# Rotary embedding of 16 x 512 x 1024: rows of a tile taken in pairs, tables on a second queue, the last tile stored whole

## The chip, the cores and the metric

One core of a Trainium2 chip. The metric is the device time of one execution in microseconds (us); lower is better. A run over 1.5% above the fastest of its kernel counts as slow and is left out of the ratios. "DVE" is the vector engine, "Pool" in the profile is GpSimd, "ACT" is ScalarE, "PE" the tensor engine and "SP" the engine that issues most transfers. Sixteen DMA engines move the data.

## The reference

```python
batch, seq, dim = 16, 512, 1024        # float32, 16 heads of 64
x1, x2 = x[..., :32], x[..., 32:]      # per head
out = concatenate([x1 * cos - x2 * sin, x1 * sin + x2 * cos], axis=-1)
# cos and sin: [512, 32], the same for all batches and heads
```

In and out are 33.55 MB each; the tables are 64 KB each.

## The kernel before

A tile is two batches: 128 partitions with eight sequence rows of 1024 values each, 4 MB. There are eight tiles and five buffers. Each output row is `x * cos + swapped(x) * sin`, where `swapped` exchanges the halves of each head and the sign is in the table. DVE makes the cosine product into PSUM, GpSimd the sine product into SBUF (`b`), and DVE adds the two. In two of the eight rows PE adds instead, by a product with the identity, and ScalarE copies the sum out; for row 0 DVE makes the sine product too.

```python
FIRST = (3, 8); LAST_OUT = (4, 8); SMALL = (15, 14, 12, 8)
PE_ROWS = ((0, 4), (0, 4)); DVE_B = ((0,), (0,))

load(0, 0, FIRST[0])                                # all on SP's queue
nc.sync.dma_start(out=sin_sb, in_=sin_v)
nc.sync.dma_start(out=cos_sb, in_=cos_v)
for lo, hi in zip(FIRST, FIRST[1:]): load(0, lo, hi)
for t in range(1, BUFS): load(t)
# ... tables spread over 128 partitions by PE, then into `sns` by DVE ...

for t in range(NT):
    for k in range(KK):                             # one row of 1024 at a time
        if not own:   nc.gpsimd.tensor_tensor(out=halves(b), in0=swapped(r, nh), in1=over_heads(sk), op=ALU.mult)
        if k in PE_ROWS[t % 2]:
            # two cosine products of 512, [own: one sine product on DVE], two PE additions, two ACT copies
        else:
            nc.vector.tensor_tensor(out=pairs(ps), in0=pairs(r), in1=cos_b(k, 2 * nh), op=ALU.mult)
            pending.append((r, ps, b))              # later: r = ps + b on DVE
        if k == 0 and t > 0: finish(t - 1)          # sums, then the store on SP's queue
    if t == NT // 2 - 1: # four tiny loads on ScalarE's queue that nothing uses
finish(NT - 1)                                      # last tile: rows 0-3, then rows 4-7
```

SP issues all loads and stores of `x` in the order loads 0 to 4, stores 0 to 2, loads 5 to 7, stores 3 to 7.

## Time and profile before

| | before |
|---|---|
| time, median of 3 runs | 162.39 us (162.34 to 162.41) |
| span of the profile | 160.7 us |
| moved by the main queue | 67.24 MB, in use 97.9% of the span |
| DVE busy, Pool busy | 141.4 us, 130.3 us |
| DVE on data | 10.75 to 151.88 us |
| last store issued, landed | 151.96, 159.8 us |

How to read it: ask first which resource has no idle time from beginning to end. A high busy share is not enough; DVE is busy 88% and is idle only at the ends, yet it has finished almost 9 us before the span does. The lines of the profile that carry this are in the prediction.

### The profile page before, as it was taken

The page shows a single profiled execution, that of the slowest core. Times are in us where ns is not written, and L with a number is a line of the kernel's source. Part 1 is how long each engine was busy: PE and PEld are TensorE (multiplying, and loading weights), DVE is VectorE, ACT ScalarE, POOL GpSimd, SP SyncE. Part 2 cuts the span into 40 slices and gives each one's busy share as a digit, 9 for nine tenths or more (in the row PEclk, how much of TensorE's full clock was granted, in tenths as well). Part 3 has the DMA queues.
Part 4 walks back from the last instruction along what each step waited for, and adds up shares of the span by engine and source line. Part 5 has one row for each costly group of instructions (what it writes and reads, how often), then busy time and mean ns, then how long its engine had stood idle before and what let it go on. Part 6 is the DMA issues. An engine that isn't in the chain of part 4 may idle for free. (4 is left out here: it accounts for less than half of the span.)

```text
span 160.7 us, 531 instructions
## 1 busy us (share of the span) xinstructions
PE 62.1 (39%) x71; PEld 20.0 (12%) x71; DVE 141.4 (88%) x142; ACT 20.0 (12%) x33; POOL 130.3 (81%) x62
## 2 busy tenths in 40 slices
PE   3146370536217250709045540918063722735000
PEld 0112010202011110202020200211020201120000
DVE  1059999999999999999999999999999999999800
ACT  0201120021102020111102020202001110202000
POOL 1039999999999999999999899999999799940000
PEclk9999958576956776595555555555555585587655
DMA  5999999999999999999999999999999999999994
GB/s 190 398 408 473 392 490 424 392 481 432 392 432 473 394 432 473 400 400 498 408 400 465 441 400 434 457 416 424 465 408 424 473 408 416 465 416 412 416 432 192
DMA packets 2852, 67.26 MB, mean 419 GB/s; under 512 B 418, under 2 KB 546, under 8 KB 546
## 3 DMA queue, kind: packets, MB, share of 16 engines
q1 hardware_dynamic: 2752, 67.24, 97.9%
q10 hardware_dynamic: 98, 0.00, 0.0%
q14 instruction: 2, 0.02, 0.0%
HBM read 33.69 MB, written 33.55 MB: 419 GB/s over the span
## 5 line engine op out<-in xcount | busy, mean ns | idle before, releaser
L168 POOL TENSOR_TENSOR b<-xt,sns 128x1024 f32<-128x1024 f32 x56 | 129.6, 2354 | 11.6 <-DVE sns L111 9.2
L186 DVE TENSOR_TENSOR pd<-xt,tab 128x1024 f32<-128x1024 f32 x48 | 58.1, 1225 | 0.8
L148 DVE TENSOR_TENSOR xt<-pd,b 128x1024 f32<-128x1024 f32 x48 | 58.3, 1217 | 0.0
L181 PE MATMUL ps<-xt,ident 128*128 128x512 f32 x32 | 29.6, 1082 | 49.0 <-issue 38.4
L181 PE MATMUL ps<-b,ident 128*128 128x512 f32 x32 | 29.0, 1061 | 29.6 <-DVE ps L174 27.0
L182 ACT COPY xt<-ps 128x512 f32<-128x512 f32 x32 | 18.7, 585 | 120.4 <-PE ps L181 120.4
L174 DVE TENSOR_TENSOR ps<-xt,tab 128x512 f32<-128x512 f32 x32 | 20.6, 687 | 0.0
L181 PEld LDWEIGHTS ps<-xt,ident 128*128 128x128 f32 x32 | 9.4, 324 | 68.3 <-issue 63.7
L181 PEld LDWEIGHTS ps<-b,ident 128*128 128x128 f32 x32 | 9.2, 316 | 49.6 <-issue 25.6
L179 DVE TENSOR_TENSOR xt<-xt,tab 128x1024 f32<-128x1024 f32 x8 | 9.8, 1221 | 0.4
L110 DVE TENSOR_SCALAR sns<-tab 128x256 f32<-128x256 f32 x1 | 0.4, 425 | 8.1 <-PE tab L108 8.1
L107 PE MATMUL tab<-b,spread 64*128 64x256 f32 x2 | 1.2, 697 | 5.0 <-DMA b<-in_sin_dram 5.0
L182 ACT ACT_TABLE_LOAD x1 | 1.3, 1283 | 7.1 <-DMA xt<-in_x_dram 7.1
L97 PE MATMUL ps<-zero 128*128 128x512 bf16 x3 | 1.5, 623 | 1.2 <-DVE zero L94 1.2
L107 PEld LDWEIGHTS tab<-b,spread 64*128 64x128 f32 x2 | 0.5, 306 | 5.9 <-issue 5.9
L108 PE MATMUL tab<-b,spread 64*128 64x256 f32 x2 | 1.1, 632 | 0.0
L94 DVE MEMSET zero<- 128x256 uint32 x1 | 0.3, 272 | 0.9 <-PEq L211 0.9
L108 PEld LDWEIGHTS tab<-b,spread 64*128 64x128 f32 x2 | 0.7, 334 | 0.2
L106 DVE COPY spread<-ident 64x64 f32<-64x64 f32 x2 | 0.3, 182 | 0.2 <-POOL ident masks.py:199 0.2
L97 PEld LDWEIGHTS <-zero 128*128 128x128 bf16 x3 | 0.3, 124 | 1.5 <-DVE zero L94 1.2
masks.py:197 POOL MEMSET ident<- 128x128 f32 x1 | 0.2, 204 | 0.3 <-POOLq L211 0.3
L111 DVE COPY sns<-tab 128x256 f32<-128x256 f32 x1 | 0.4, 414 | 0.0
(6 smaller groups left out, 0.9 us busy)
## 6 DMA issues: line engine op xcount, KB each, us to landing
xt<-in_x_dram SPq DMA_DIRECT2D x7, 4096.0 KB, 29.1
out_dram<-xt SPq DMA_DIRECT2D x7, 4096.0 KB, 27.8
out_dram<-xt SPq DMA_DIRECT2D x2, 2048.0 KB, 8.4
xt<-in_x_dram SPq DMA_DIRECT2D x1, 2560.0 KB
xt<-in_x_dram SPq DMA_DIRECT2D x1, 1536.0 KB, 6.3
b<-in_sin_dram SPq DMA_DIRECT2D x1, 64.0 KB, 6.3
b<-in_cos_dram SPq DMA_DIRECT2D x1, 64.0 KB, 6.1
spare<-in_sin_dram ACTq DMA_DIRECT2D x1, 0.9 KB, 5.7
```

The source lines that it names most:

```text
L97: nc.tensor.matmul(out=ps, lhsT=zero[:, :P], rhs=zero, start=True, stop=True)
L107: nc.tensor.matmul(out=sin_t, lhsT=spread, rhs=sin_sb, start=True, stop=True)
L108: nc.tensor.matmul(out=cos_t, lhsT=spread, rhs=cos_sb, start=True, stop=True)
L110: nc.vector.tensor_scalar_mul(out=sns[:, :, 0, :], in0=sin_k, scalar1=-1.0)
L111: nc.vector.tensor_copy(out=sns[:, :, 1, :], in_=sin_k)
L148: nc.vector.tensor_tensor(out=r, in0=ps, in1=b, op=ALU.add)
L168: nc.gpsimd.tensor_tensor(out=halves(b), in0=swapped(r, nh), in1=over_heads(sk), op=ALU.mult)
L174: nc.vector.tensor_tensor(out=pairs(ps), in0=pairs(rc), in1=cos_b(k, BANK // half), op=ALU.mult)
L179: nc.vector.tensor_tensor(out=halves(r), in0=halves(r), in1=swapped_signed(k), op=ALU.mult)
L181: nc.tensor.matmul(out=ps, lhsT=ident, rhs=rhs, start=False, stop=True, skip_group_check=True)
L182: nc.scalar.copy(out=rc, in_=ps)
L186: nc.vector.tensor_tensor(out=pairs(ps), in0=pairs(r), in1=cos_b(k, 2 * nh), op=ALU.mult)
```

## The change

The intent: fewer, longer instructions on DVE and GpSimd (six of eight rows in pairs), tables that needn't wait behind the first load, and one transfer less at the end. The diff, cut to its core ("..." marks a cut; the comments are added here):

```diff
-B_BUFS = 6
-PE_ROWS = ((0, 4), (0, 4))
-DVE_B = ((0,), (0,))
-FIRST = (3, 8)
-LAST_OUT = (4, 8)
-SMALL = (15, 14, 12, 8)
+ROW_OWN, ROW_PE = 0, 3
+PAIRS = ((1, 2), (4, 5), (6, 7))
+FIRST = (2, 3, 8)
+LAST_OUT = (8,)
+EXTRA = 4
...
-    nc.sync.dma_start(out=sin_sb, in_=sin_v)
-    nc.sync.dma_start(out=cos_sb, in_=cos_v)
+    nc.scalar.dma_start(out=sin_sb, in_=sin_v)
+    nc.scalar.dma_start(out=cos_sb, in_=cos_v)
...
+    spare = fixed.tile([1, EXTRA, 16], FP32)
+    for i in range(EXTRA):
+        nc.sync.dma_start(out=spare[:1, i], in_=sin_v[:1, :16])
...
+    cos_product(own_ps, rows(0, ROW_OWN), ROW_OWN)
     for t in range(NT):
-        for k in range(KK):                      # one row at a time ... (cut)
+        first, second, third = PAIRS
+        b1 = sin_rows(t, first[0], 2)            # GpSimd, 2048 elements
+        p1 = pair_product(t, first[0])           # DVE, 2048 elements
+        r0 = rows(t, ROW_OWN)
+        own_product(r0)                          # DVE, 1024
+        for ps, r in zip(parts(own_ps), parts(r0)):
+            pe_add(ps, swapped(r))
+        nc.scalar.copy(out=r0, in_=own_ps)
+        b3 = sin_rows(t, ROW_PE, 1)
+        b2 = sin_rows(t, second[0], 2)
+        pair_sum(*p1, b1)                        # DVE, 2048
+        h0, h1 = zip(parts(rows(t, ROW_PE)), parts(b3))
+        pe_half(ROW_PE, *h0)                     # DVE 512, PE, ACT
+        p2 = pair_product(t, second[0])
+        b1 = sin_rows(t, third[0], 2)
+        pair_sum(*p2, b2)
+        pe_half(ROW_PE, *h1)
+        p1 = pair_product(t, third[0])
+        if t + 1 < NT:
+            cos_product(own_ps, rows(t + 1, ROW_OWN), ROW_OWN)
+        pair_sum(*p1, b1)
+        stores(t)
```

The buffers for `b` become three of twice the size, and the sum of each row 0 is made in one PSUM tile of 1024.

More of the change, by code (lines that the diff above doesn't have):

```diff
@@ L61 @@
     xp = ctx.enter_context(tc.tile_pool(name="xp", bufs=BUFS))
-    bp = ctx.enter_context(tc.tile_pool(name="bp", bufs=B_BUFS))
+    bp = ctx.enter_context(tc.tile_pool(name="bp", bufs=3))
     pfix = ctx.enter_context(tc.tile_pool(name="pfix", bufs=1, space=bass.MemoryType.PSUM))
-    pe = ctx.enter_context(tc.tile_pool(name="pe", bufs=3, space=bass.MemoryType.PSUM))
-    pd = ctx.enter_context(tc.tile_pool(name="pd", bufs=2, space=bass.MemoryType.PSUM))
+    pe = ctx.enter_context(tc.tile_pool(name="pe", bufs=1, space=bass.MemoryType.PSUM))
+    pd = ctx.enter_context(tc.tile_pool(name="pd", bufs=1, space=bass.MemoryType.PSUM))
     ctx.enter_context(tc.manual_schedule())
@@ L81 @@
     load(0, 0, FIRST[0])
-    sin_sb = bp.tile([P, dim], FP32, name="b")[:PB, : KK * half]
-    cos_sb = bp.tile([P, dim], FP32, name="b")[:PB, : KK * half]
-    nc.sync.dma_start(out=sin_sb, in_=sin_v)
-    nc.sync.dma_start(out=cos_sb, in_=cos_v)
+    tabs = bp.tile([P, 2 * dim], FP32, name="b")
+    sin_sb = tabs[:PB, : KK * half]
+    cos_sb = tabs[:PB, dim : dim + KK * half]
+    nc.scalar.dma_start(out=sin_sb, in_=sin_v)
+    nc.scalar.dma_start(out=cos_sb, in_=cos_v)
     for lo, hi in zip(FIRST, FIRST[1:]):
@@ L94 @@
     nc.vector.memset(zero, 0.0)
-    for i in range(3):
-        ps = pe.tile([P, BANK], FP32, name="ps")
+    own_ps = pe.tile([P, dim], FP32)
+    pe_ps = pe.tile([P, BANK], FP32)
+    for ps in (own_ps[:, :BANK], own_ps[:, BANK:], pe_ps):
         nc.tensor.matmul(out=ps, lhsT=zero[:, :P], rhs=zero, start=True, stop=True)
-    spare = fixed.tile([16, len(SMALL), 16], FP32)
     sns = fixed.tile([P, KK, 2, half], FP32)
@@ L104 @@
     spread = fixed.tile([PB, P], FP32)
-    for b in range(NB):
-        nc.vector.tensor_copy(out=spread[:, b * PB : (b + 1) * PB], in_=ident[:PB, :PB])
+    eye = ident[:PB, :PB]
+    nc.vector.tensor_copy(
+        out=spread.rearrange("p (b q) -> p b q", b=NB),
+        in_=bass.AP(tensor=eye.tensor, offset=eye.offset, ap=[eye.ap[0], [0, NB], [1, PB]]),
+    )
     nc.tensor.matmul(out=sin_t, lhsT=spread, rhs=sin_sb, start=True, stop=True)
@@ L111 @@
     nc.vector.tensor_copy(out=sns[:, :, 1, :], in_=sin_k)
-    on_dve = sorted(set(DVE_B[0]) | set(DVE_B[1]))
-    sns_t = tab[:, KK * half : KK * half + len(on_dve) * hd]
-    for i, k in enumerate(on_dve):
-        nc.vector.tensor_copy(out=sns_t[:, i * hd : (i + 1) * hd], in_=sns[:, k])
-    def cos_b(k, n):
-        c = cos_t[:, k * half : (k + 1) * half]
-        return bass.AP(tensor=c.tensor, offset=c.offset, ap=[c.ap[0], [0, n], [1, half]])
-    def over_heads(s):
-        return bass.AP(tensor=s.tensor, offset=s.offset, ap=[s.ap[0], [0, nh], [1, hd]])
@@ L124, in swapped @@
-    def swapped(r, n):
-        return bass.AP(
-            tensor=r.tensor, offset=r.offset + half, ap=[r.ap[0], [hd, n], [-half, 2], [1, half]]
-        )
-    def swapped_signed(k):
-        i = on_dve.index(k)
-        s = sns_t[:, i * hd : (i + 1) * hd]
-        return bass.AP(
-            tensor=s.tensor, offset=s.offset + half, ap=[s.ap[0], [0, nh], [-half, 2], [1, half]]
-        )
-    def pairs(r):
-        return r.rearrange("p (a j) -> p a j", j=half)
-    def halves(r):
-        return r.rearrange("p (h a j) -> p h a j", a=2, j=half)
@@ L143, with heads, swapped @@
-    pending = []
-    def add(most):
-        while len(pending) > most:
-            r, ps, b = pending.pop(0)
-            nc.vector.tensor_tensor(out=r, in0=ps, in1=b, op=ALU.add)
-    def finish(t):
-        add(0)
+    own_t = tab[:, KK * half : KK * half + hd]
+    nc.vector.tensor_copy(out=own_t, in_=sns[:, ROW_OWN])
+    def heads(r):
+        return r.rearrange("p (h a j) -> p h a j", a=2, j=half)
+    def swapped(r):
+        n = r.shape[1] // hd
+        return bass.AP(tensor=r.tensor, offset=r.offset + half, ap=[r.ap[0], [hd, n], [-half, 2], [1, half]])
@@ new lines, in rows, with cos_product @@
+    def rows(t, k, n=1):
+        return tiles[t][:, k * dim : (k + n) * dim]
+    def cos_product(out, r, k, n=1):
+        c = cos_t[:, k * half : (k + n) * half]
+        m = r.shape[1] // (n * half)
+        if n == 1:
+            cb = bass.AP(tensor=c.tensor, offset=c.offset, ap=[c.ap[0], [0, m], [1, half]])
+            o, i = (z.rearrange("p (a j) -> p a j", j=half) for z in (out, r))
+        else:
+            cb = bass.AP(tensor=c.tensor, offset=c.offset, ap=[c.ap[0], [half, n], [0, m], [1, half]])
+            o, i = (z.rearrange("p (k a j) -> p k a j", k=n, j=half) for z in (out, r))
+        nc.vector.tensor_tensor(out=o, in0=i, in1=cb, op=ALU.mult)
@@ new lines, in own_product, with sin_product @@
+    def own_product(r):
+        s = bass.AP(
+            tensor=own_t.tensor,
+            offset=own_t.offset + half,
+            ap=[own_t.ap[0], [0, nh], [-half, 2], [1, half]],
+        )
+        nc.vector.tensor_tensor(out=heads(r), in0=heads(r), in1=s, op=ALU.mult)
+    def sin_product(out, r, k, n):
+        s = sns[:, k : k + n].rearrange("p k a j -> p (k a j)")
+        if n == 1:
+            sb = bass.AP(tensor=s.tensor, offset=s.offset, ap=[s.ap[0], [0, nh], [1, hd]])
+            o, i = heads(out), swapped(r)
+        else:
+            sb = bass.AP(tensor=s.tensor, offset=s.offset, ap=[s.ap[0], [hd, n], [0, nh], [1, hd]])
+            o = out.rearrange("p (k h a j) -> p k h a j", k=n, a=2, j=half)
+            i = bass.AP(
+                tensor=r.tensor,
+                offset=r.offset + half,
+                ap=[r.ap[0], [dim, n], [hd, nh], [-half, 2], [1, half]],
+            )
+        nc.gpsimd.tensor_tensor(out=o, in0=i, in1=sb, op=ALU.mult)
@@ new lines, in sin_rows, with parts, pe_add, pe_half @@
+    def sin_rows(t, k, n):
+        b = bp.tile([P, 2 * dim], FP32, name="b")[:, : n * dim]
+        sin_product(b, rows(t, k, n), k, n)
+        return b
+    def parts(r):
+        return [r[:, i * BANK : (i + 1) * BANK] for i in range(r.shape[1] // BANK)]
+    def pe_add(ps, other):
+        nc.tensor.matmul(out=ps, lhsT=ident, rhs=other, start=False, stop=True, skip_group_check=True)
+    def pe_half(k, r, b):
+        cos_product(pe_ps, r, k)
+        pe_add(pe_ps, b)
+        nc.scalar.copy(out=r, in_=pe_ps)
@@ L152, in finish, with pair_product, pair_sum, stores @@
+    def pair_product(t, k):
+        ps = pd.tile([P, 2 * dim], FP32, name="pd")
+        cos_product(ps, rows(t, k, 2), k, 2)
+        return ps, rows(t, k, 2)
+    def pair_sum(ps, r, b):
+        nc.vector.tensor_tensor(out=r, in0=ps, in1=b, op=ALU.add)
+    def stores(t):
         lo = 0
@@ L158, in finish @@
                 load(n)
+    cos_product(own_ps, rows(0, ROW_OWN), ROW_OWN)
     for t in range(NT):
-        xt = tiles[t]
-        for k in range(KK):
-            r = xt[:, k * dim : (k + 1) * dim]
-            own = k in DVE_B[t % 2]
-            if not own:
-                b = bp.tile([P, dim], FP32, name="b")
-                sk = sns[:, k].rearrange("p a j -> p (a j)")
-                nc.gpsimd.tensor_tensor(out=halves(b), in0=swapped(r, nh), in1=over_heads(sk), op=ALU.mult)
-            if k in PE_ROWS[t % 2]:
-                parts = []
-                for c in range(0, dim, BANK):
-                    ps = pe.tile([P, BANK], FP32, name="ps")
-                    rc = r[:, c : c + BANK]
-                    nc.vector.tensor_tensor(
-                        out=pairs(ps), in0=pairs(rc), in1=cos_b(k, BANK // half), op=ALU.mult
-                    )
-                    parts.append((ps, rc, swapped(rc, BANK // hd) if own else b[:, c : c + BANK]))
-                if own:
-                    nc.vector.tensor_tensor(out=halves(r), in0=halves(r), in1=swapped_signed(k), op=ALU.mult)
-                for ps, rc, rhs in parts:
-                    nc.tensor.matmul(out=ps, lhsT=ident, rhs=rhs, start=False, stop=True, skip_group_check=True)
-                    nc.scalar.copy(out=rc, in_=ps)
-            else:
-                add(1)
-                ps = pd.tile([P, dim], FP32, name="pd")
-                nc.vector.tensor_tensor(out=pairs(ps), in0=pairs(r), in1=cos_b(k, 2 * nh), op=ALU.mult)
-                pending.append((r, ps, b))
-            if k == 0 and t > 0:
-                finish(t - 1)
-            add(1)
@@ L191 @@
-        if t == NT // 2 - 1:
-            for i, n in enumerate(SMALL):
-                nc.scalar.dma_start(out=spare[:n, i], in_=sin_v[:n, :16])
-    finish(NT - 1)
+        first, second, third = PAIRS
[7 more added lines that the diff above has]
+        b3 = sin_rows(t, ROW_PE, 1)
```

## The prediction

> **What bounds the kernel now.** I read the slices of the page first, then its queues and memory traffic, then the busy time of the engines in chosen stretches, then the queue's own waits, and the groups of instructions last. Two engines are busy over 80% of the span, so the page alone could suggest a compute bound. The rows of the transfers decide otherwise:
>
> ```profile
> DVE  1059999999999999999999999999999999999800
> POOL 1039999999999999999999899999999799940000
> DMA  5999999999999999999999999999999999999994
> q1 hardware_dynamic: 2752, 67.24, 97.9%
> q14 instruction: 2, 0.02, 0.0%
> HBM read 33.69 MB, written 33.55 MB: 419 GB/s over the span
> ```
>
> DVE starts in the third slice and stops two slices before the end; the transfers fill all forty, the first and last in part. One queue carries 67.24 MB and is in use 97.9% of the span. The same cut into two stretches (columns: span, then busy us of PE, PEld, DVE, ACT, POOL, then granted clock, DMA share, GB/s):
>
> ```profile
> 1.70:157.70 156.00, 61.63 (x71) 19.78 (x69) 140.85 (x139) 20.01 (x33) 129.60 (x56) 0.66 1.00 429
> 157.70:160.70 3.00, 0.00 (x0) 0.00 (x0) 0.00 (x0) 0.00 (x0) 0.00 (x0) 0.50 0.24 104
> ```
>
> For 156 of 160.7 us the DMA share is 1.00, with no hole. What is left is about 1.7 us before the first byte and the 3 us end, in which engines that lag finish and the last store is confirmed. The stores wait for compute, yet this does not cost time:
>
> ```profile
> SPq L79 <- DVE xt L148: 125.2, 9, 23.9
> SPq L75 <- DMA out_dram<-xt: 14.5, 2, 9.5
> SPq L225 <- DMA out_dram<-xt: 7.3, 2, 4.8
> ```
>
> The issuing engine waited 125.2 us for sums, but work already queued kept the DMA share at 1.00. The last two half stores show by how much compute is ahead. They were issued at 146.04 and 151.96 us, and landed 9.0 and 7.9 us later:
>
> ```profile
> out_dram<-xt SPq DMA_DIRECT2D x1, 2048.0 KB, 9.0
> ```
>
> ```profile
> 151.96 0.33 SPq L79 DMA_DIRECT2D out_dram<-xt  x1
> out_dram<-xt SPq DMA_DIRECT2D x1, 2048.0 KB, 7.9
> ```
>
> Landings at 155.0 and 159.8, 4.8 us apart, are 2.10 MB at 435 GB/s: the second half streamed right behind the first. The packet records agree: packets of the last tile begin at 148.6 us, directly behind those of the store before. So a store of the whole tile has to reach the DMA engines by 148.6 us, or a hole opens.
>
> ```profile
> L168 POOL TENSOR_TENSOR b<-xt,sns 128x1024 f32<-128x1024 f32 x56 | 129.6, 2354 | 11.6 <-DVE sns L111 9.2
> L186 DVE TENSOR_TENSOR pd<-xt,tab 128x1024 f32<-128x1024 f32 x48 | 58.1, 1225 | 0.8
> L148 DVE TENSOR_TENSOR xt<-pd,b 128x1024 f32<-128x1024 f32 x48 | 58.3, 1217 | 0.0
> L174 DVE TENSOR_TENSOR ps<-xt,tab 128x512 f32<-128x512 f32 x32 | 20.6, 687 | 0.0
> L179 DVE TENSOR_TENSOR xt<-xt,tab 128x1024 f32<-128x1024 f32 x8 | 9.8, 1221 | 0.4
> ```
>
> DVE is the slower compute engine, with hardly any idle time (0.8 us) once it has begun at 10.75 us. It ends at 151.88 us: 141.1 us for 8 tiles, 17.64 us each. The transfers take 155.6 us for the same tiles, 19.4 each.
>
> [...] The trace has 429 over 156 us, 432 in its middle[...]. The trace has 687 and 1217 to 1226[...]. The trace has 2354 for 1024; its doubling is 4708. I use 4.6 us as an estimate.
>
> **The change part by part.**
>
> *Pairs on DVE.* Consecutive instructions overlap. Starts in the timeline are about 1.135 us apart for 1024 elements and 0.60 for 512, and some 0.1 more where one waits for the result or buffer of the one before. Check against before: 13 x 1.135 + 4 x 0.60 = 17.16, plus about five such waits, 0.5: 17.66, measured 17.64. The same slope gives 1.135 + 1024 x 0.535/512 = 2.205 us for 2048 elements. After, a tile has three pair products and three pair sums (6 x 2.205 = 13.23), two instructions of 1024 (2.27), two of 512 (1.20), and about three dependent neighbours (0.3): 17.0 us. Six instructions become three in each kind; 0.6 us per tile, 5 us in all. None of it lies on the path that sets the end.
>
> *Pairs on GpSimd.* Three pairs at 4.6 and one row at 2.35: 16.15 us per tile, as before (7 x 2.32 = 16.2), and under DVE's 17.0. In the first tile the sum of the second pair must wait: tables multiplied from 8.5, first pair until 13.1, row 3 after its piece lands (about 13.7) until 16.0, second pair until 20.6, while DVE is ready at about 18. So 2.6 us are lost there once.
>
> *Tables on ScalarE's queue.* Before, they sat behind 1.5 MB and landed at 1.17 + 6.3 = 7.5 and 1.74 + 6.1 = 7.8 us; the two table products ended at 9.7, and DVE began on data at 10.75. [...] I expect them by about 5.2 and 6.4, and DVE on data at about 8.7. Their bytes are the same.
>
> *End of compute.* 8.7 + 8 x 17.0 + 2.6, less 0.5 since the first product needs no GpSimd work: about 147 us, against 151.9. The whole store is then issued at about 147.0. At the start of before the first issue at 0.73 us put a first packet at 1.75, 1.0 us later, so packets could begin at about 148.0, and the place in line is at 148.6. It just fits, with 0.6 us to spare.
>
> *First tile in 2, 1 and 5 rows; last store whole.* Bytes are unchanged. The records have 1213 ns for a 32 KB packet and 611 for one of 16 KB; eight packets per DMA engine make 8 x (2 x 611 - 1213) = 0.07 us saved. [...] The four tiny loads at the start replace four tiny ones in the middle: nothing.
>
> *Instruction fetches.* Two 8 KB instruction packets arrive at 54.2 and 97.8 us; next to them a data packet took 1.70 or 1.53 us instead of 1.21, after about 0.3 us idle. Two DMA engines end at 159.34 and 159.38 us where the others end between 158.3 and 159.0. This lag, 0.4 to 0.5 us, fits them. DVE's and PE's streams shrink by over a third (DVE's arithmetic from 17 to 10 per tile, matmuls from 8 to 4), so I expect one or both fetches to go: about 0.4 us on the path.
>
> Sum on the path that sets the end: -0.4 (fetches), -0.1 (packets), 0 from all arithmetic: 162.39 becomes 161.9 us.
>
> **The rivals.** First: compute gains come through, because DVE at 88% sets the pace; 5 us less would give about 157.5. Against it: DMA share 1.00 in the stretch above, and 67.24 MB at 432 GB/s are 155.6 us whatever the engines do. I give it almost nothing. Second: the store of the whole last tile comes too late. If DVE ends at 149 instead of 147, a hole of about 1.4 us opens and the time is about 163.3; if at 151 or later (patterns with one more dimension run slower, or GpSimd becomes the bound at over 18 us per tile), 165 or more. For it: only 0.6 us of reserve by my sum, whose parts are uncertain by a microsecond or two. Against it: pair operations have the same elements in the same order, and DVE's slack in the middle is 2.4 us per tile. Third: the start shifts[...] and the first bytes come 0.3 us later or earlier; that adds to the end one to one. Fourth: nothing changes at all, 162.4, if the fetches stay.
>
> **Range and chances.** Centre 161.9. Nothing visible gives more than 0.7 us, so the low end is 161.2. The high end, 163.0, allows a hole of about 1 us at the end. A gain of over 2% needs 3.2 us from a stream that has no hole: 0.01. A loss of over 2% needs DVE to end around 151: 0.03. Within 2%: 0.96.
>
> **What would show it right or wrong.** The slices of the changed kernel should again show DMA at 9 throughout, and 1.00 in a long stretch. [...] DVE should begin data at 8 to 9 us and end near 147. The store of the last tile should be issued before about 147.6, and the stretch from 147 to 151 should have no dip of DMA share. The row of instruction packets should have fewer than two. The prediction is wrong if the DMA share dips in the last 15 us, if a pair on GpSimd takes over 5.2 us, or if the stream itself moves at another rate with the same bytes.

Marked gaps in the text above are statements about the hardware that no trace of this case shows. The sum: 162.39 less 0.4 (fetches) and 0.1 (packets) is 161.9. The 0.1 is the 0.07 us of the larger packets, rounded. Between the gaps, 429 and 432 are GB/s, 687 and 1217 to 1226 are ns of DVE for 512 and 1024 elements, and 2354 is ns of GpSimd for 1024. The 4.6 us for a pair on GpSimd was the estimate, a little under the doubling of 2354; with 4.71 the first tile would wait 0.1 us longer, and a tile would take GpSimd 16.5 us, still under DVE's 17.0. The tables' 5.2 and 6.4 us, and with them the 8.7 us of the start, were the author's estimate and not shown by a trace; they enter the sum only through its zero for the arithmetic (the store issued in time, at 147.0).

## The result, and the profile after

On one chip, side by side: before 162.40 us (median of 4, 162.34 to 162.44), after 162.37 us (median of 4, 162.20 to 162.48). The ratio is 0.9998, with a 95% interval from 0.9980 to 1.0015: no difference. Ratios here and below are the mean time of one kernel's fast runs over that of the other's in the same rounds, so not quite the ratio of the medians that stand beside them.

From the page of the kernel after: slices, queues and traffic.

```profile
DVE  1079879999999999999999999999999999997000
POOL 1059999999999999988998799989989899830000
DMA  5999999999999999999999999999999999999993
q1 hardware_dynamic: 2600, 67.11, 97.8%
q10 hardware_dynamic: 160, 0.13, 0.3%
q14 instruction: 1, 0.01, 0.0%
HBM read 33.69 MB, written 33.55 MB: 419 GB/s over the span
```

DVE now stops three slices ahead of the end instead of two. The row of the transfers is the same but for one digit. The main queue carries 0.13 MB less, which are the tables, now on the other queue; one instruction packet is left of two. The long stretch of the kernel after (columns as in the prediction):

```profile
1.70:157.70 156.00, 56.49 (x71) 17.88 (x69) 135.77 (x83) 18.66 (x25) 126.40 (x32) 0.64 1.01 431
```

DVE does 5.1 us less work (140.85 to 135.77), and the transfers have no hole, before or after. The groups of the kernel after, different shapes kept apart:

```profile
L165 POOL TENSOR_TENSOR b<-xt,sns 128x2048 f32<-128x2048 f32 x24 | 108.3, 4520 | 14.0 <-DVE sns L117 8.6 <-DVE xt L189 4.3 <-DMA xt<-in_x_dram 1.2
L189 DVE TENSOR_TENSOR xt<-pd,b 128x2048 f32<-128x2048 f32 x24 | 54.9, 2287 | 2.4 <-POOL b L165 1.6
...
L165 POOL TENSOR_TENSOR b<-xt,sns 128x1024 f32<-128x1024 f32 x8 | 18.8, 2351 | 0.0
```

A pair takes 4520 ns on GpSimd and 2287 on DVE. DVE waited 1.6 us for GpSimd, once. The waits of the issuing engine, kernel after:

```profile
SPq L78 <- DVE xt L189: 112.2, 7, 16.6
SPq L74 <- DMA out_dram<-xt: 16.7, 2, 9.7
SPq L254 <- DMA out_dram<-xt: 11.4, 2, 9.6
```

It waited 13 us less for sums (125.2 to 112.2) and got 4.1 us of it back as a longer wait for the last stores to land (7.3 to 11.4). The last store of the kernel after, first in its timeline (start and duration of the issue), then in the list of issues of the stretch from 140 us (count, size, us to landing):

```profile
147.59 0.33 SPq L78 DMA_DIRECT2D out_dram<-xt  x1
```

```profile
out_dram<-xt SPq DMA_DIRECT2D x1, 4096.0 KB, 12.0
```

It was issued 4.37 us earlier than the last half store before (151.96) and landed at 159.6 against 159.8. The four microseconds went into standing in line.

### The profile page after: what moved, and what is told of

Read it like the earlier page. It is cut to its first block, busy times and chain, and to the rows that moved or that the text cites. A ratio compares the mean times of both kernels' runs of the same rounds, so it can differ in the third digit from the quotient of the medians.

```text
span 160.4 us, 444 instructions
## 1 busy us (share of the span) xinstructions
PE 57.0 (36%) x71; PEld 18.1 (11%) x71; DVE 136.3 (85%) x85; ACT 18.7 (12%) x25; POOL 127.1 (79%) x38
## 3 DMA queue, kind: packets, MB, share of 16 engines
q1 hardware_dynamic: 2600, 67.11, 97.8%
## 4 chain that ended last, share of the span: by engine, by line
DVE 68%; issue 11%; POOL 7%; DMA 4%; PE 1%; ACTq 0%; DVEq 0%
DVE xt L189 33%; DVE pd L141 31%; POOL b L165 7%; DMA b<-in_cos_dram 4%; DVE pe_ps L141 4%; PE tab L114 1%; ACTq L84 0%; DVE sns L116 0%; DVE xt L150 0%; DVE own_ps L141 0%; DVE sns L117 0%; DVEq L189 0%
## 5 line engine op out<-in xcount | busy, mean ns | idle before, releaser
L165 POOL TENSOR_TENSOR b<-xt,sns 128x2048 f32<-128x2048 f32 (+1 forms) x32 | 126.4, 3978 | 14.0 <-DVE sns L117 8.6
L189 DVE TENSOR_TENSOR xt<-pd,b 128x2048 f32<-128x2048 f32 x24 | 54.9, 2287 | 2.4 <-POOL b L165 1.6
L141 DVE TENSOR_TENSOR pd<-xt,tab 128x2048 f32<-128x2048 f32 x24 | 55.0, 2292 | 0.2
L176 PE MATMUL own_ps<-xt,ident 128*128 128x512 f32 x32 | 30.1, 1095 | 59.4 <-DVE xt L150 53.7
L176 PE MATMUL pe_ps<-b,ident 128*128 128x512 f32 x32 | 24.7, 864 | 22.6 <-DVE pe_ps L141 22.6
L176 PEld LDWEIGHTS own_ps<-xt,ident 128*128 128x128 f32 x32 | 9.4, 324 | 75.2 <-DVE xt L150 60.5
L209 ACT COPY xt<-own_ps 128x1024 f32<-128x1024 f32 x8 | 8.1, 1012 | 78.6 <-PE own_ps L176 78.6
L181 ACT COPY xt<-pe_ps 128x512 f32<-128x512 f32 x16 | 9.4, 586 | 32.8 <-PE pe_ps L176 32.8
L141 DVE TENSOR_TENSOR pe_ps<-xt,tab 128x512 f32<-128x512 f32 x16 | 11.0, 685 | 0.0
L141 DVE TENSOR_TENSOR own_ps<-xt,tab 128x1024 f32<-128x1024 f32 x8 | 9.8, 1223 | 0.0
```

Of the source, the lines that this page charges most:

```text
L141: nc.vector.tensor_tensor(out=o, in0=i, in1=cb, op=ALU.mult)
L165: nc.gpsimd.tensor_tensor(out=o, in0=i, in1=sb, op=ALU.mult)
L176: nc.tensor.matmul(out=ps, lhsT=ident, rhs=other, start=False, stop=True, skip_group_check=True)
L181: nc.scalar.copy(out=r, in_=pe_ps)
L189: nc.vector.tensor_tensor(out=r, in0=ps, in1=b, op=ALU.add)
L209: nc.scalar.copy(out=r0, in_=own_ps)
```

## The experiments

All were timed against the kernel before in the same rounds on the same chip. All results were correct except those of the two that leave out the work.

### How late may the last store be?

**The kernel before with its last tile whole.**

```diff
-LAST_OUT = (4, 8)
+LAST_OUT = (8,)
```

> The kernel before, with its last tile stored whole instead of in two halves. Theory S (the DMA stream sets the time, and compute matters only where a transfer is issued after its place in line): DVE still ends at about 151.9 us, the store is issued at about 152.0 and its first packet starts 1.0 us later, at 153.0, where its place in line began at 148.6. A hole of about 4.4 us opens, the DMA share falls in the stretch from 149 to 153, and the time is 166 to 167 us. Rival C (compute sets the pace, the store's form is a detail): within 1 us of 162.4.

Measured: 165.85 us against 162.51 (ratio 1.020, interval 1.0184 to 1.0217). Its last store in the timeline:

```profile
152.17 0.33 SPq L79 DMA_DIRECT2D out_dram<-xt  x1
```

The stretch from 148 to 154 us in the kernel before, in this one, and for comparison in the kernel after (columns as in the prediction: DMA share and GB/s last):

```profile
148.00:154.00 6.00, 0.00 (x0) 0.00 (x0) 3.84 (x4) 0.00 (x0) 0.00 (x0) 0.67 0.94 401
```

```profile
148.00:154.00 6.00, 0.00 (x0) 0.00 (x0) 4.07 (x4) 0.00 (x0) 0.00 (x0) 0.65 0.26 109
```

```profile
148.00:154.00 6.00, 0.00 (x0) 0.00 (x0) 0.00 (x0) 0.00 (x0) 0.00 (x0) 0.50 0.99 426
```

The hole is there: the DMA share falls from 0.94 to 0.26. The kernel after, with a whole store too, has none (0.99). Rival C falls, but the 166 to 167 that Theory S asked for was a little too much. The packet records tell why. The sixteen DMA engines ended the store before between 148.65 and 149.90 us, and all resumed at 153.0, 0.83 us after the issue. The time moved by 3.3 us, which is close to what the *slowest* engine waits (3.1 us) and not to what the first does (4.4 us). (I use one long stretch here because a packet's bytes are counted where it starts: with packets of 1.2 us, stretches of 1 us jump up and down even where nothing is idle.)

**The changed kernel with 2.4 us more work on DVE before its last sum,** with the store whole and in halves.

```diff
         if t + 1 < NT:
             cos_product(own_ps, rows(t + 1, ROW_OWN), ROW_OWN)
+        else:
+            for _ in range(2):
+                cos_product(own_ps, rows(t, third[0]), third[0])
         pair_sum(*p1, b1)
```

> The changed kernel with two extra cosine products of 1024 elements on DVE in the last tile, ahead of its last sum (results unchanged): DVE ends about 2.4 us later and the whole store is issued near 150.0 us instead of 147.6. Theory S with the reserve that I read in the trace (packets could start at about 148.6, place in line from 148.7 to 149.5): reserve 0.1 to 0.6 us, so 1.8 to 2.3 us are added: 164.2 to 164.7. If the reserve were 2 us or more the time would stay at 162.4 to 162.8. Rival C (DVE's end sets the end one to one): 164.8.

> The same two extra products, with the last tile stored in halves. Theory S: DVE ends just as late, but the first half is in the queue by about 145 us and covers until about 153.5, the second half issued near 150.0 is in time: 162.4 us within 0.3, so the delay of DVE costs nothing. Rival C (DVE's end sets the end): 164.8, the same as with the whole store.

Measured: whole 163.55 us (ratio 1.0061, interval 1.0035 to 1.0087), in halves 162.49 (0.9999, interval 0.9979 to 1.0019), before 162.51. The same stretch of both, whole first:

```profile
148.00:154.00 6.00, 0.00 (x0) 0.00 (x0) 1.92 (x1) 0.00 (x0) 0.00 (x0) 0.50 0.64 273
```

```profile
148.00:154.00 6.00, 0.00 (x0) 0.00 (x0) 1.75 (x1) 0.00 (x0) 0.00 (x0) 0.50 0.92 393
```

The pair is the cleanest answer. The same work ends DVE at 149.92 and 149.75 us; with halves in the queue it costs nothing, with one whole store it opens a hole. But the hole cost 1.0 us and not the 1.8 to 2.3 that I expected. The slowest engine ended the store before at 149.81 and resumed at 150.81: 1.0 us. So the reserve has to be counted from the slowest engine.

**The same with one extra product instead of two,** to test just that reading.

> The changed kernel with one extra cosine product of 1024 elements on DVE in the last tile: the whole store is issued 1.1 to 1.2 us later, near 148.8, and can start at 149.8. Theory L (the slowest DMA engine sets the end, the others may idle until it is done): it is free at 149.5 to 149.8, so 0 to 0.3 us are added, 162.4 to 162.7 us, although the fastest engines idle 1 us. Rival P (the reserve of my prediction, counted from the first engine at 148.6 to 148.7): 1.0 us is added, 163.4.

Measured: 162.68 us against 162.34 (ratio 1.0014, interval 0.9998 to 1.0030). Theory L holds and P falls: the store was issued at 149.12, the first engines had been free since 148.94, yet the slowest was busy until 149.60 and the first new packet started at 149.95, 0.35 us later. In the records the completions of all engines then lie within 0.13 us of each other, where the changed kernel has 0.82: after this idle stretch the engines were in line again.

**The changed kernel with its last tile in halves again.**

```diff
-LAST_OUT = (8,)
+LAST_OUT = (4, 8)
```

> The changed kernel with its last tile stored in two halves again, nothing else undone. Theory S: no hole before and none now, so 162.4 us within 0.3; the first half is issued near 145 us and gives some 2 us of reserve that nothing uses. Rival H (the whole store opens a small hole at the end which ate the gain that was forecast): 0.4 us or more faster, 162.0 or less.

Measured: 162.87 us against 162.51 (ratio 1.0019, interval 1.0003 to 1.0034). Rival H falls, as it is not faster. It is 0.17 us above the band of Theory S, and why is not settled: in its trace one DMA engine ended 1.0 us after all others (159.91 against 158.92), while the kernel with the same transfers and *more* work (late, in halves) had 162.49. I read it as the lag of single DMA engines that the next part is about, not as a cost of the halves. That isn't shown; as all four of its runs lie between 162.66 and 163.04, it isn't chance from run to run alone.

### What sets the last half microsecond?

**Loads and stores alone** (wrong result): the changed kernel without any work on the tiles.

```diff
-    cos_product(own_ps, rows(0, ROW_OWN), ROW_OWN)
     for t in range(NT):
-        ...
         stores(t)
```

> The changed kernel with all work on the tiles taken away: every tile is loaded and stored as it is, in the same transfers and order; the result is wrong on purpose. Theory S: the stream is the same, so at most what fetches, lagging engines and the start cost goes away: 161.6 to 162.4 us, DMA share 1.00 from 1.7 to 157.7 us, no instruction packet during the run, and last packets that end close together. Rival C (compute sets the pace or takes memory bandwidth from the transfers): 158 us or less.

Measured: 161.79 us against 162.37 (ratio 0.9965, interval 0.9953 to 0.9977). From its page, and its long stretch (no ACT column, as ScalarE did nothing there):

```profile
DMA  5999999999999999999999999999999999999995
q1 hardware_dynamic: 2600, 67.11, 98.0%
HBM read 33.69 MB, written 33.55 MB: 420 GB/s over the span
```

```profile
1.70:157.70 156.00, 3.35 (x7) 1.03 (x5) 0.98 (x3) 0.00 (x0) 1.00 1.01 431
```

This bounds what arithmetic can cost with these transfers: without any, the kernel is 0.6 us faster. Rival C (158 or less) is gone. There is no row of instruction packets, and the last packets end close together.

How far the slowest of the sixteen DMA engines lags the median engine at five points, from the records of the packets by which each engine reports the end of its share (us; not a view of the profile). At 52 us the first loads end, at 62 and 81 the first and third store, at 110 the last load:

```
                    at 52   at 62   at 81   at 110   at the end   instruction packets at
before               0.30    0.69    0.69    0.73      0.72        54.2, 97.8
after                0.30    0.23    0.55    0.60      0.60        78.6
after, run again     0.27    0.19    0.66    0.81      0.59        79.8
after, in halves     0.23    0.22    0.86    1.29      1.27        79.9
loads and stores     0.26    0.25    0.24    0.26      0.26        none
```

The median engine reports its end at 158.5 to 158.7 us in all five; it is the slowest that differs. In the four with work on the tiles its lag jumps by 0.3 to 0.6 us after the first instruction packet, some at the turn from loads to stores near 110 us. The jump follows the packet and not the turn between loads and stores: the kernel before jumps between 52 and 62 and not at 81, the other three the other way round. In the kernel before the slowest engine stays behind from 110 us to the end, with a lag of 0.72 us at every report. Between the first and the last of the sixteen engines there were 0.4 us at 42 us in the kernel before; before the last store 0.65 to 1.65 us in the twelve traces with work on the tiles and 0.39 without; and 0.13 to 0.16 us after a stretch in which all were idle.

The packet records show more. They name no engine, but the packets of one engine follow each other without a gap, so the sixteen chains can be put together. In the kernel before, the instruction packet at 54.25 us fills one engine's chain for 0.32 us, and the data packet right behind it takes 1.70 us instead of 1.21. That engine goes from 0.09 us ahead of the median to 0.68 behind, and it ends last, at 159.38. The packet at 97.78 (0.31 us, then a data packet of 1.53) takes another engine from 0.26 ahead to 0.34 behind; it ends near 159.0. The engine that ends at 159.34 carried no instruction packet; from 110 us on it falls back by 0.07 to 0.09 us with each whole store, and why is open. In all twelve traces with work on the tiles an instruction packet takes 0.31 or 0.32 us and the data packet behind it 1.45 to 1.70: 0.55 to 0.80 us of one engine's time. So it is shown that the engine which carries the packet is set back. What that costs the kernel depends on where this engine stood before.

**More instruction packets:** the changed kernel with 240 one-element copies on ScalarE.

```diff
         pe_half(ROW_PE, *h1)
+        for i in range(30):
+            nc.scalar.copy(out=junk[:, i : i + 1], in_=ident[:, i : i + 1])
```

> The changed kernel with 240 one-element copies on ScalarE, thirty in each tile where ScalarE is idle: the only aim is more instruction packets. Theory F (an instruction packet holds up one DMA engine by 0.5 to 0.8 us, and the end waits for the slowest): two or more further packets, each with a data packet of over 1.5 us beside it, and last packets that end 0.3 to 0.8 us later; 162.5 to 163.1 us. Rival N (the lag of single engines is noise, or is made up by the spread of the others): 162.4 us within 0.15.

Measured: the six runs were 162.55, 162.88 and 163.25 us, and 167.10, 167.78 and 167.96, which are slow runs and are left out (the median of all six, 165.17, means nothing). All four slow runs belong to the two kernels with extra copies, three here and one in the next experiment, so the copies may bring them about, and this ratio may show less than their whole cost; the granted clock is hardly lower in the three (0.635 to 0.643 against 0.645 to 0.649). The ratio of the fast runs is 1.0032, interval 1.0014 to 1.0049. The row of its page:

```profile
q14 instruction: 3, 0.02, 0.0%
```

Three instruction packets, a spread of the engines of 1.44 us before the last store, the last data packet at 160.30 us, 1.1 us after that of the kernel after: Theory F's direction, its time within the band, its last packet beyond the 0.8 us that it allowed. But the turn from loads to stores at 50 us also cost 0.73 us per engine here against 0.27 in the kernel after, so the two aren't apart in the time. By the chains, the packets at 80.02 and 105.86 set two different engines back by 0.6 to 0.7 us each, and the second of these ends last.

**The same into loads and stores alone,** to take the rest of the work out of the comparison.

```diff
+    for i in range(300):
+        nc.scalar.copy(out=junk[:, i % 32 : i % 32 + 1], in_=ident[:, i % 32 : i % 32 + 1])
     for t in range(NT):
         stores(t)
```

> Load and store alone (wrong on purpose), with 300 one-element copies on ScalarE that nothing waits for; they bring instruction packets into a run that had none. Theory F (each instruction packet holds up one DMA engine by about 0.35 us, and the end waits for the slowest engine, so several packets on different engines cost no more than one): three or more packets, lags of 0.3 to 0.4 us that appear at their times, end spread 0.6 to 1.0 us against 0.39 without, and 162.0 to 162.5 us against 161.8. Rival N (the lag has another source, such as the compute engines' accesses): spread 0.4 and 161.8 as without.

Measured: 163.91 us against 162.34 (fast runs' ratio 1.0099, interval 1.0074 to 1.0124). Neither theory gave that: the fast runs lie at 163.7 to 164.9 us, about 2 us above loads and stores alone (161.79, on another chip). The only trace of it fell in a slow run (168.88 us), from which no cause may be read. The experiment is inconclusive; it brought in something larger than what it was to measure.

**The changed kernel without its four tiny loads.**

```diff
-    spare = fixed.tile([1, EXTRA, 16], FP32)
-    for i in range(EXTRA):
-        nc.sync.dma_start(out=spare[:1, i], in_=sin_v[:1, :16])
```

> The changed kernel without the four tiny loads at the end of the loads. The question is the turn from loads to stores at 50 us, where 13 packets of the changed kernel took over 1.23 us (0.27 us per DMA engine lost against 0.05 before). Theory E (the tiny loads, queued there on one DMA engine, disturb the turn): the slow packets go and the time falls by 0.1 to 0.3, to 162.1 to 162.3. Rival T (it is the turn itself, and differs from run to run): slow packets as before, 162.4 within 0.15.

Measured: 162.72 us against 162.37 (ratio 1.0016, interval 1.0004 to 1.0028). Theory E falls, and 162.72 is outside Theory T's band too: 30 slow packets at the turn instead of 13, 0.54 us per engine lost instead of 0.27. The turn is slow without these loads as well, and differs from run to run. Loads and stores alone also lose 0.22 us there, with 13 slow packets, so the work on the tiles isn't needed for it. Whether the tiny loads help, and why, is open. In this run DVE also began late (10.96 us) and the store was issued at 148.46.

### What is the tables' own queue worth?

**The kernel before with the tables on ScalarE's queue** and the first tile in two, one and five rows.

```diff
-FIRST = (3, 8)
+FIRST = (2, 3, 8)
...
-    nc.sync.dma_start(out=sin_sb, in_=sin_v)
-    nc.sync.dma_start(out=cos_sb, in_=cos_v)
+    nc.scalar.dma_start(out=sin_sb, in_=sin_v)
+    nc.scalar.dma_start(out=cos_sb, in_=cos_v)
```

> The kernel before with the tables on ScalarE's queue and the first tile in pieces of two, one and five rows, nothing else. DVE should start on data at about 10.1 us as in the changed kernel, against 10.75, and end at about 151.2. Theory S: 162.4 us within 0.2, as the store in halves was in time already. Rival C: 0.6 us faster, 161.8.

Measured: 162.71 us against 162.37 (ratio 1.0020, interval 1.0007 to 1.0033). It is not faster, so rival C falls; it is even 0.3 us slower, outside Theory S's band. DVE began on data at 11.37 us, not at 10.1: the cosine table came later than without the change. The late start itself is unlikely to be the 0.3 us, by my estimate: DVE began at 10.09 us in the changed kernel and at 10.73 in the next experiment, and both ratios to the kernel before are within 0.0002 of 1. In the trace, that of the slowest of the five runs, the slowest engine lags the median by 1.4 us at the end (160.00 against 158.60). But most of the 0.3 us lies outside the span: the five runs are 1.96 to 2.03 us longer than their spans, where all other runs are 1.73 to 1.84. The spans themselves have a median of 160.7 us, against 160.6 for the kernel before in the same rounds. So within the span Theory S holds; what lengthens the rest by 0.2 us is open.

**The changed kernel with the tables back on SP's queue** (and the first tile in three and five rows).

> The changed kernel with the tables back on the same queue as the tiles and the first tile in pieces of three and five rows, as before. The tables land at 7.5 and 7.8 us as before and DVE starts on data at about 10.8, against 10.1 (between 9.9 and 11.1 in five traces of this change). Theory S: DVE ends near 148.2, the store is at most 0.2 us late for the slowest engine: 162.3 to 162.6 us. Rival (the tables' own queue is worth its 2 us): 163.5 or more.

Measured: 162.37 us against 162.34 (ratio 0.9999, interval 0.9981 to 1.0016). DVE began at 10.73 and ended at 148.16 us, as forecast: Theory S. The queue of their own is worth nothing to the time.

**The changed kernel again.**

> The changed kernel as it is, to have it on the same chip as the three beside it. 162.2 to 162.6 us, ratio to before 0.998 to 1.002. One instruction packet near 79 us; the slowest DMA engine's last packet 0.4 to 0.8 us behind the median engine's, which ends at 158.6.

Measured: 162.28 us against 162.34 (ratio 0.9999, interval 0.9979 to 1.0020); single runs from 162.22 to 163.18. In this trace DVE began at 10.57 and the store was issued at 148.08, so its first engines idled; the time was no worse. A second time, no difference.

## Why the prediction was right or wrong

**The bound: right.** The forecast was 161.9 us, 161.2 to 163.0, and within 2% at 0.96; the measured 162.37 lies in it, and the direction of its small gain was not borne out. The stream sets the time. After, the DMA share is 1.01 over 156 us (1.00 before); with no arithmetic the time is 161.79 us. DVE's 5 us were real (140.85 to 135.77 in the stretch) and were spent in line.

**Pairs: right.** Forecast 17.0 us of DVE per tile; the stores of tiles 5 and 6 were issued at 114.57 and 131.54, 16.97 apart. Pairs took 2287 and 2292 ns on DVE and 4520 on GpSimd (4600 used). No cost of the extra dimension shows: a straight line through the kernel before's 687 ns for 512 elements and 1217 to 1225 for 1024 gives 2277 to 2301 for 2048 on DVE (my estimate), and on GpSimd the doubling of 2354 is 4708.

**The tables: wrong by more than a microsecond.** The step that failed is "I expect them by about 5.2 and 6.4". It rested on an assumption that the trace below contradicts: that the tables would move from the start beside the first piece. From the timelines, before first, then after:

```profile
7.62 1.19 PE L107 MATMUL tab<-b,spread 64*128 64x256 f32 x2 [4.97 <-DMA b<-in_sin_dram]
...
9.70 0.42 DVE L110 TENSOR_SCALAR sns<-tab 128x256 f32<-128x256 f32 x1 [8.08 <-PE tab L108]
```

```profile
0.73 0.54 ACTq L84 DMA_DIRECT2D b<-in_sin_dram  x1
...
6.04 1.19 PE L113 MATMUL tab<-b,spread 64*128 64x256 f32 x2 [3.40 <-DMA b<-in_sin_dram]
...
7.78 1.22 PE L114 MATMUL tab<-b,spread 64*128 64x256 f32 x2 [0.55 <-DMA b<-in_cos_dram]
9.03 0.42 DVE L116 TENSOR_SCALAR sns<-tab 128x256 f32<-128x256 f32 x1 [7.47 <-PE tab L114]
```

The sine table was used at 6.04 and the cosine table, on which the start hangs, at 7.78, where before both were there by about 7.8. DVE began at 10.09 instead of 8.7, and between 9.93 and 11.37 in the other traces with this part. The list of queues in two stretches of the kernel after, 0.7 to 4.6 us and 4.6 to 7 us, shows what happened:

```profile
q1 hardware_dynamic: 118, 0.97, 74.0%
```

```profile
q1 hardware_dynamic: 184, 0.91, 101.7%
q10 hardware_dynamic: 160, 0.13, 17.1%
```

The sine table was issued at 0.73 us, in the same moment as the first piece. In the first 3.9 us the second queue moved nothing, not one packet of 160. The records have its first packet at about 4.8 us, when the first of the DMA engines is through its rows of the first piece (the first piece ends at 5.18; each engine's share of it is 8 rows and a report, 9 records of the trace). That each engine ended its rows of the first piece before it took up the tables fits these times; it was not tested by itself, and why the second queue had to wait is not shown.

**The wait of the first tile: 1.6 us, not 2.6.** GpSimd's late start was shared by DVE. This error and the last cancel: 1.4 us later start, 1.0 us less wait, and DVE ended at 147.53 where 147 was forecast. Right for partly wrong reasons.

**The reserve at the end: mis-sized.** "It just fits, with 0.6 us to spare" counted from the first DMA engine to come free. Counted so, even less was left: issued at 147.59 and not 147.0, and with 0.83 us instead of 1.0 to the first packet, the store could start at 148.42, 0.3 us before the first engine was free (148.71). But the time is set by the slowest, which was free at 149.53, 1.1 us after 148.42. The two late kernels put it at 1.2 to 1.35 us: issued 2.39 us later than in the kernel after, the one cost 1.04; issued 1.53 us later, the other cost 0.34. Both are differences of medians with the scatter of 0.3 us on them. The rival with the hole was right in kind: it is the kernel before with a whole store.

**The instruction packets: the step that gave the forecast gain failed.** "So I expect one or both fetches to go: about 0.4 us on the path." One went. Part of the premise was a miscount: PE has 71 instructions before and 71 after in the first rows of the pages, so of the two that it named only DVE's shrank (142 to 85). And the arithmetic was wrong. The prediction gave both late ends, 159.34 and 159.38 us, to the two packets; by the chains only 159.38 belongs to one of them, the engine of the other ended near 159.0, and its "about 0.3 us idle" is the instruction packet itself. The end is the latest of sixteen, so as long as one packet is left its engine can still end last: in the kernel after, the packet at 78.59 us takes its engine to 0.6 behind the median, as far as the chains can be told apart there, and the last data packet moved only from 159.38 to 159.20. In the timed runs nothing is left of it (0.9998). So the measured time is that of the fourth rival, "nothing changes at all, 162.4", although its condition, that the fetches stay, held for one of two.

**The rest.** The tiny loads and the number of pieces could be neglected to within 0.2%: without the loads the ratio was 1.0016, and with two pieces and the tables back on SP's queue 0.9999. No measured time contradicts the stream's bound; in the traces the last data packet accounts for 0.48 of the 0.6 us that separate the real kernel from loads and stores alone (159.20 against 158.72). What stays open is how fetches, turns and other disturbances share in it.

## What to carry to other kernels

Here one queue was in use for 97.8% of the span, and 5 us less work on DVE left the time as it was (0.9998). It only showed in *how late a store may be issued*: the last one was issued 4.37 us earlier, and that let the kernel drop the last store in halves, a step that cost the kernel before 3.3 us (165.85 against 162.51). Where you find one queue full from end to end, ask for this reserve. Count it from the slowest DMA engine (1.2 to 1.35 us here, against 0.3 from the first to come free), and test it by adding a known delay on both sides of it. And ask of a delay that strikes one of the sixteen engines whether that engine ends last: of the two instruction packets before, one belonged to the engine that ended last, at 159.38 us, the other to one that ended near 159.0; one of two went, the last data packet moved by 0.18 us (159.38 to 159.20), and in the timed runs nothing was left of it.
